# The up projection of a ConvFFN by Strassen's algorithm in a hybrid diffusion layer

## Chip, cores and metric

The kernel runs on one core of one Trainium2 chip. The metric is the device time of one execution in microseconds. Three runs of the kernel before have the median 1294.14 us (lowest 1293.99).

## What is computed

One layer of a diffusion backbone for 128 context tokens and 512 latent tokens, T = 640 columns in all: a combined input projection, latent attention beside a bidirectional state-space scan, their gated sum and an output projection, then a ConvFFN and a final norm. All numbers are fp32. The ConvFFN is the part that the change touches:

```
h2 = rmsnorm(x, lp['norm_ffn_g']) * (1 + sc2) + sh2
u = dwconv_centred(h2 @ lp['w_up'], lp['ffn_conv_w'], lp['ffn_conv_b'])
x = x + g2 * ((jax.nn.silu(u[..., :D_FF]) * u[..., D_FF:]) @ lp['w_down'])
```

with D_MODEL = 1024 and D_FF = 2816. The convolution has width 3 and runs along the tokens, within the context and within the latent tokens.

## The kernel before

Everything is feature-major: a tile has 128 features on the partitions and the 640 tokens as columns. A "page" is such a tile, 128x640.

**Products.** TensorE multiplies in the type fp32r. For accuracy each operand is split into a high and a low part, and `mm3` (L124) adds three products: high x high, high x low, low x high. `split` (L104) makes the parts: ScalarE (ACT) casts to the high part (L105), and VectorE (DVE) or GpSimd (POOL) subtracts it (`sub`, L101, shown in the profile as L102) for the low part. A product over 640 columns takes two matmuls, of 384 and 256 columns (`halves`, L131).

**Weights.** `wload` (L117) loads a raw weight tile of 128x1024 from the SP queue into one of four raw buffers and splits it, the low part on POOL, into one of two buffer pairs.

**ConvFFN, up.** w_up has 44 tiles of output features, in 22 pairs of a gate tile and a value tile. The loop (L1184) goes over the pairs. A tile is 8 steps of the contraction x 3 products x 2 halves = 48 matmuls into one PSUM buffer `big` of two banks (two such buffers); one value comes from `early_part` (L1165), a tile of the second pair that is computed ahead of its turn and lies in SBUF. `conv` (L451) evacuates: one ACT operation with the middle tap and the bias (L453), then four DVE operations for the two outer taps (L455, L458), of 127 and 511 columns, which read PSUM and the page they add to. Then ACT does SiLU (L1200), DVE multiplies the two halves (L1201) and `split` makes the two parts of the activation, which stay in SBUF (pools `fl`, `fr`).

**ConvFFN, down.** For each of 8 output tiles (L1209) 22 steps x 3 products x 2 halves = 132 matmuls are accumulated, and `residual` (L1090) adds the scaled result to x, which was parked in DRAM (`scr_x`). The last tile is done in two column parts (L1237), followed by the final norm and the stores.

**Ahead of it.** `h2_part` (L1142) makes the normed and modulated h2 in place in the tiles `x1` (fp32), and splits it into the pages `h2`, 16 of the 21 pages of pool `pg`.

**Order.** A planner orders the instructions of every engine by their priority in program order and by estimated durations; each engine then runs its own list strictly in that order. Only within `tc.manual_schedule` is the named engine's list the program order. DMAs of the weights, of x and of parked tiles all go through the SP queue.

Of the kernel before, what the change touches and what calls it, by code (L numbers as in the profile page):

```python
# [38 lines left out]
# steps of the streams of products with h between the parts of the attention (F_) and of the SSD (G_)  # L39
FILL0, F_R0, F_A0 = 16, 3, 4  # L40
F_S, F_P, F_R, F_Q, F_K = (0, 1, 1, 2), 1, 1, 1, 2
# start: buffers of modulation weights, and which feature tiles go to which engine at which step
# [9 lines left out]
# SSD: share of the other engines, buffers, and where the parts of decays() run  # L52
# [7 lines left out]
RP = 2  # L60
LAG, F_T, F_V = 2, (1, 2), (1, 0, 1, 1, 1)

# columns of the per-feature vector table
# [8 lines left out]
def trunk_kernel(ctx: ExitStack, tc: tile.TileContext, a: dict):  # L72
# [9 lines left out]
    def nm(s):  # L82
        uid[0] += 1
        return f"{s}{uid[0]}"
# [39 lines left out]
    def mm3(outs, hi, lo, rhs, first, last):  # L124
        """outs: list of (psum AP, column slice of the moving operand); rhs = (hi, lo)"""
        plan = [(hi, rhs[0]), (hi, rhs[1]), (lo, rhs[0])]
        for i, (w, r) in enumerate(plan):
            for o, s in outs:
                PE.matmul(o, w, r[:, s], start=first and i == 0, stop=last and i == 2)  # L129
# [20 lines left out]
    def sumsq(sqs, c):  # L150
        """PSUM column i: the sum over the features of the squares of token tile i of the columns c"""
# [17 lines left out]
    def rstd_rows(ps, n, c):  # L169
        """1 / rms of the tokens of the columns c on every partition, in PSUM; ps from sumsq"""  # L170
# [9 lines left out]
    def sqrt_table(x):  # L180
        """has the table of Sqrt loaded once x is there"""
# [4 lines left out]
    def rstd_full(sq, n, out, dg):  # L186
        """out [128, T]: 1 / rms from the sums of squares; dg: scratch [128, T]"""
# [7 lines left out]
    def add_sq(acc, x, sq):  # L195
        """acc + x * x"""
# [5 lines left out]
    def row_sums(stat, raws, m=128):  # L202
        """four partial sums each of the products of the columns stat (two rows, padded to 32) with the tiles raws"""
# [19 lines left out]
    def col_sums(ps, sb, m, n):  # L223
        """the partial sums added, feature-major"""
# [7 lines left out]
    def ada_rows(tiles, tile, nraw):  # L232
        """modulation columns by row products on the elementwise engines; tile(n) makes a [128, n] tile.
        tiles: the feature tiles. Returns a function that issues the next one of them behind an instruction of DVE"""
# [20 lines left out]
    def scale_col(out, sc, g):  # L255
        """(1 + sc) * g of one feature tile"""
        DVE.tensor_scalar(out, sc, 1.0, vec[:, g : g + 1], ALU.add, ALU.mult)

# [1 line left out]
    # the first columns of h @ w_in come from x * gain * (1 + scale) alone: the rms factors of the tokens and the  # L260
# [1126 lines left out]
```

## Time and profile before

| | |
|---|---|
| median of the runs | 1294.14 us |
| span of the profiled execution | 1293.0 us, 20744 instructions |
| PE (TensorE matmuls) busy | 1230.2 us, 95%, 8361 matmuls |
| PEld (weight loads) busy | 1165.6 us, 90% |
| DVE busy | 725.3 us, 56% |
| ACT busy | 542.7 us, 42% |
| POOL busy | 497.8 us, 38% |
| mean granted clock of TensorE | 0.975 |

The span runs from the first to the last instruction on the chip; some 1.1 us of the measured time lie outside it. Busy shares are averages over stages with different limits. An instruction that has started but is held up by something that no semaphore shows counts as busy, so that a mean duration can contain waiting. In the forms of the rows `128x640 f32<-128x640 f32` gives partitions x elements of output and input, and names such as `wlo<-raw,whi` the tiles written and read. `[2.30 <-DVE pg L458]` behind a row of the timeline is the idle time before it and what ended it.

### The profile page before, as it was taken

What the parts mean: (1) busy time and instruction counts of PE and PEld (TensorE: products, weight loads), DVE (VectorE), ACT (ScalarE), POOL (GpSimd) and SP (SyncE); (2) the same over time, 40 slices, a digit from 0 to 9 for tenths busy, and PEclk for the clock granted to TensorE, in tenths of its full rate; (3) what the DMA queues carried; (4) which work ended last, traced back from release to release, by engine and by line L of the source; (5) the groups of instructions that cost most, each with busy time, mean ns of one, the idle gap of its engine ahead of it and who ended that gap; (6) DMA issues with size and microseconds to landing.
All of it is one profiled execution on the core that took longest, in us unless ns stands there. A gap on an engine that the chain in (4) does not pass through costs nothing. (4 is left out here: it accounts for less than half of the span.)

```text
span 1293.0 us, 20744 instructions
## 1 busy us (share of the span) xinstructions
PE 1230.2 (95%) x8361; PEld 1165.6 (90%) x8361; DVE 725.3 (56%) x1285; ACT 542.7 (42%) x943; POOL 497.8 (38%) x260
## 2 busy tenths in 40 slices
PE   7798999999999889899989899999999999999997
PEld 5698999989999888788888898899999999999997
DVE  4767555564546895777788988744443443400003
ACT  5455454544547516535573231433333333311220
POOL 3433021221222236945577554323233332334450
PEclk9999999999999899999999988999999999999999
DMA  8333221222117764122356574121222222242212
GB/s 326 128 102 98 70 76 54 76 70 81 52 64 262 252 223 164 48 78 88 105 191 229 182 250 163 35 82 66 82 72 76 82 66 82 64 152 81 81 48 82
DMA packets 53680, 148.23 MB, mean 115 GB/s; under 512 B 6224, under 2 KB 11792, under 8 KB 53584
## 3 DMA queue, kind: packets, MB, share of 16 engines
q1 hardware_dynamic: 51824, 144.80, 33.3%
q10 hardware_dynamic: 1760, 2.11, 0.6%
q8 instruction: 66, 1.08, 0.4%
q14 instruction: 30, 0.25, 0.1%
HBM read 124.01 MB, written 20.35 MB: 112 GB/s over the span
## 5 line engine op out<-in xcount | busy, mean ns | idle before, releaser
L129 PE MATMUL big<-pg,whi 128*128 128x384 f32 (+1 forms) x3752 | 729.4, 315 | 6.6 <-DVE pg L1083 4.0
L129 PEld LDWEIGHTS big<-pg,whi 128*128 128x128 f32 x3752 | 572.2, 191 | 25.5 <-issue 16.4
L102 POOL TENSOR_TENSOR wlo<-raw,whi 128x1024 fp32r<-128x1024 f32 (+1 forms) x128 | 321.0, 2509 | 606.5 <-ACT whi L105 594.6
L129 PE MATMUL big<-pg,wlo 128*128 128x384 f32 (+1 forms) x1876 | 436.1, 312 | 6.5 <-POOL wlo L102 6.3
L129 PEld LDWEIGHTS big<-pg,wlo 128*128 128x128 f32 x1876 | 292.6, 191 | 8.4 <-POOL wlo L102 7.8
L105 ACT CAST whi<-raw 128x1024 fp32r<-128x1024 f32 (+2 forms) x133 | 135.1, 1016 | 189.4 <-PE big L129 169.1
L455 DVE SCALAR_TENSOR_TENSOR st<-big,vec,st 128x127 f32<-128x127 f32 x68 | 37.0, 544 | 105.3 <-ACT st L453 105.3
L105 ACT CAST pg<-pg 128x640 fp32r<-128x640 f32 x46 | 33.0, 727 | 106.6 <-DVE pg L1201 67.1
L1094 DVE SCALAR_TENSOR_TENSOR pg<-big,mod,pg 128x128 f32<-128x128 f32 (+2 forms) x15 | 7.5, 543 | 122.9 <-PE big L129 122.9
L129 PE MATMUL sm<-pg,whi 128*128 128x384 f32 (+1 forms) x256 | 63.0, 327 | 5.4 <-ACT pg L105 3.9
L102 DVE TENSOR_TENSOR pg<-pg,pg 128x640 fp32r<-128x640 f32 x43 | 41.1, 963 | 23.8 <-ACT pg L105 23.8
L129 PEld LDWEIGHTS sm<-pg,whi 128*128 128x128 f32 x256 | 46.0, 197 | 8.2 <-ACT pg L105 4.3
L250 DVE SCALAR_TENSOR_TENSOR araw<-araw,crow 128x1024 f32<-128x1024 f32 x32 | 52.6, 1645 | 0.4
L584 ACT ACTIVATE p<-sm,st 128x320 f32<-128x320 f32 x64 | 33.2, 524 | 44.7 <-DVE st L582 44.7
L455 DVE SCALAR_TENSOR_TENSOR pg<-big,vec,pg 128x127 f32<-128x127 f32 (+1 forms) x42 | 22.9, 545 | 51.4 <-ACT pg L453 51.4
L581 DVE TENSOR_REDUCE st<-sm 128x1 f32<-128x320 f32 (+1 forms) x72 | 31.6, 464 | 35.8 <-PE sm L577 35.7
L102 DVE TENSOR_TENSOR ptl<-sm,pth 128x512 fp32r<-128x512 f32 (+1 forms) x48 | 29.6, 621 | 37.1 <-ACT pth L600 37.0
L250 DVE SCALAR_TENSOR_TENSOR junk<-araw,crow 128x1024 f32<-128x1024 f32 x32 | 47.0, 1470 | 0.0
L600 ACT CAST pth<-sm 128x512 fp32r<-128x512 f32 (+1 forms) x48 | 25.5, 533 | 45.1 <-PE sm L597 44.9
L129 PE MATMUL sm<-pg,wlo 128*128 128x384 f32 (+1 forms) x128 | 41.3, 322 | 0.0
L458 DVE SCALAR_TENSOR_TENSOR st<-big,vec,st 128x127 f32<-128x127 f32 x68 | 37.2, 547 | 1.7
L998 DVE TENSOR_TENSOR k<-k,k 128x512 f32<-128x512 f32 x20 | 28.5, 1423 | 14.7 <-POOL k L997 12.6
(294 smaller groups left out, 1724.6 us busy)
## 6 DMA issues: line engine op xcount, KB each, us to landing
raw<-w_up SPq DMA_DIRECT2D x44, 512.0 KB, 3.3
araw<-w_adar SPq DMA_DIRECT2D x32, 512.0 KB, 4.6
araw<-w_ada SPq DMA_DIRECT2D x16, 512.0 KB, 7.8
raw<-w_down SPq DMA_DIRECT2D x14, 512.0 KB, 3.6
raw<-w_xbc SPq DMA_DIRECT2D x12, 512.0 KB, 3.4
raw<-w_gm SPq DMA_DIRECT2D x8, 512.0 KB, 3.3
raw<-w_o_mla SPq DMA_DIRECT2D x8, 512.0 KB, 3.4
raw<-w_z SPq DMA_DIRECT2D x8, 512.0 KB, 4.6
```

The costliest lines, as they stand in the source:

```text
L102: return eng.tensor_tensor(out, x, f(hi), ALU.subtract)
L105: ACT.copy(hi, src)
L129: PE.matmul(o, w, r[:, s], start=first and i == 0, stop=last and i == 2)
L250: DVE.scalar_tensor_tensor(out, raw, 1.0, crow[r], ALU.mult, ALU.mult, accum_out=mod[:, j, r : r + 1])
L455: DVE.scalar_tensor_tensor(dst[:, lo_ + 1 : hi_], p[:, lo_ : hi_ - 1], vec[:, w : w + 1], dst[:, lo_ + 1 : hi_], ALU.mult, ALU.add)
L458: DVE.scalar_tensor_tensor(dst[:, lo_ : hi_ - 1], p[:, lo_ + 1 : hi_], vec[:, w + 2 : w + 3], dst[:, lo_ : hi_ - 1], ALU.mult, ALU.add)
L581: DVE.reduce_max(st[:, i : i + 1], sv, AX.X)
L584: ACT.activation(p[:, i * w : (i + 1) * w], sv, AF.Exp, bias=st[:, 2:3], scale=SCALE, accum_out=st[:, 4 + i : 5 + i])
L600: return ph, pl, ACT.copy(ph[:, :n], pt[:, :n]), sub(DVE, pl[:, :n], pt[:, :n], ph[:, :n])
L998: DVE.tensor_tensor(w1, w1, e, ALU.mult)
L1094: ins = DVE.scalar_tensor_tensor(dst[:, lo_:hi_], ps[:, lo_ - cols.start : hi_ - cols.start], mod[:, gcol, r : r + 1], src[:, lo_:hi_], AL ...
```

## The change

In 20 of the 22 pairs of w_up (from the third on, `PLAIN` = 2) the product of a pair's 1024 x 256 weights with h2 is regarded as a 2x2 product of blocks: two blocks of 512 input features, two tiles of output features, and two halves of 320 tokens. Strassen's algorithm (in Winograd's form) makes the four output blocks from seven block products in place of eight. Each is 4 steps x 3 products of 320 columns, 12 matmuls.

- `t12`, `t34`: four sums of blocks of h2 (from `x1`), made once, split into pages of a pool `tt`.
- `seven(i)`: loads the two weight tiles of a pair, makes four sums of 128x512 on DVE and splits seven blocks of 128x512 (ACT cast, POOL subtraction) into buffers `sh`, `sl`, eight each. It is called one pair ahead.
- The seven products go into two banks of a `big` buffer and one bank of a `small`; products four to seven add to what an earlier product left there, after DVE or ACT has read it. Five DVE additions and two ACT copies of 320 columns make the gate tile `gt` and the value tile `vl` in SBUF pages, from which `conv` now reads.
- `gate`: after the product of the halves, the first four activations (`NKEEP`) are split into pages of the pool `xr`, which held `x1`; the next 17 go to DRAM, and the last stays as it is.
- w_down: its first three output tiles are computed together, in groups of four steps of the contraction; ahead of each group `act_split` loads the activations back and splits them. The other five tiles are as before.

```
+PLAIN, NKEEP = 2, 4
...
+    xr = ctx.enter_context(tc.tile_pool(name="xr", bufs=8))
...
-        x = hp_.tile([128, T], F32, tag="x1", name=nm("x1"), bufs=8)
+        x = page(F32, xr)
...
+    N2 = T // 2
+    lft, rgt = slice(0, N2), slice(N2, T)
+    ffn = ExitStack()
+    tt = ffn.enter_context(tc.tile_pool(name="tt", bufs=16))
+    sw = ffn.enter_context(tc.tile_pool(name="sw", bufs=1))
+    def gate(i, us):
+        ACT.activation(us[0], us[0], AF.Silu)
+        DVE.tensor_tensor(us[0], us[0], us[1], ALU.mult)
+        if i < NKEEP:
+            hi, lo = page(F32R, xr), page(F32R, xr)
+            split(hi, lo, us[0])
+            act[i] = (hi, lo)
+        elif i < NF - 1:
+            d = tc.dram_tile([128, T], F32, name=f"scr_act{i}")
+            nc.sync.dma_start(d, us[0])
+            act[i] = d
+        else:
+            act[i] = us[0]
...
+    for i in range(PLAIN):
...
+    t12, t34 = [], []
+    for k in range(4):
+        b1, b2 = x1[k], x1[4 + k]
+        ta, tb = page(), page()
+        DVE.tensor_tensor(ta[:, lft], b1[:, rgt], b1[:, lft], ALU.subtract)
+        DVE.tensor_tensor(ta[:, rgt], b2[:, rgt], ta[:, lft], ALU.subtract)
+        POOL.tensor_tensor(tb[:, lft], b2[:, rgt], b1[:, rgt], ALU.subtract)
+        DVE.tensor_tensor(tb[:, rgt], b2[:, lft], ta[:, rgt], ALU.subtract)
+        for t, out, eng in ((ta, t12, DVE), (tb, t34, POOL)):
+            hi, lo = page(F32R, tt), page(F32R, tt)
+            split(hi, lo, t, eng)
+            out.append((hi, lo))
+    def half_w():
+        return [sw.tile([128, 512], F32R, tag=t, name=nm(t), bufs=8) for t in ("sh", "sl")]
+    def part():
+        return sw.tile([128, N2], F32, tag="o3", name=nm("o3"), bufs=5)
+    def seven(i):
+        raw = []
+        for j in range(2):
+            r_ = ws.tile([128, 1024], F32, tag="raw", name=nm("raw"), bufs=RAW)
+            nc.sync.dma_start(r_, a["w_up"][2 * i + j])
+            raw.append(r_)
+        (a11, a12), (a21, a22) = ((r_[:, 0:512], r_[:, 512:1024]) for r_ in raw)
+        out = []
+        def add(x, y, op):
+            t = sw.tile([128, 512], F32, tag="sum", name=nm("sum"), bufs=4)
+            DVE.tensor_tensor(t, x, y, op)
+            return t
+        def put(x):
+            hi, lo = half_w()
+            split(hi, lo, x, POOL)
+            out.append((hi, lo))
+        put(a11)
+        s1 = add(a21, a22, ALU.add)
+        s2 = add(s1, a11, ALU.subtract)
+        put(s2)
+        put(add(a11, a21, ALU.subtract))
+        put(s1)
+        put(a12)
+        put(add(a12, s2, ALU.subtract))
+        put(a22)
+        return out
+    def product(ps, w, b, c, first):
+        for k in range(4):
+            s = slice(k * 128, (k + 1) * 128)
+            mm3([(ps, c)], w[0][:, s], w[1][:, s], b[k], first and k == 0, k == 3, not first)
+    h2a, h2b = h2[:4], h2[4:]
+    with tc.manual_schedule(engines={PE.engine}):
+        nxt = seven(PLAIN)
+        for i in range(PLAIN, NF):
+            w11, ws2, ws3, ws1, w12, ws4, w22 = nxt
+            if i + 1 < NF:
+                nxt = seven(i + 1)
+            ab, c = big(), small()[:, 0:N2]
+            pa, pb = ab[:, 0:N2], ab[:, 512 : 512 + N2]
+            gt, vl = page(), page()
+            product(pa, w11, h2a, lft, True)
+            p1 = part()
+            ACT.copy(p1, pa)
+            product(pb, ws2, t12, rgt, True)
+            u2 = part()
+            DVE.tensor_tensor(u2, pb, p1, ALU.add)
+            product(c, ws3, t34, lft, True)
+            product(pb, ws1, t12, lft, False)
+            u4 = part()
+            DVE.tensor_tensor(u4, pb, p1, ALU.add)
+            DVE.tensor_tensor(vl[:, rgt], c, u4, ALU.add)
+            product(pa, w12, h2b, lft, False)
+            ACT.copy(gt[:, lft], pa)
+            product(pb, ws4, h2b, rgt, False)
+            DVE.tensor_tensor(gt[:, rgt], pb, p1, ALU.add)
+            product(c, w22, t34, rgt, False)
+            DVE.tensor_tensor(vl[:, lft], c, u2, ALU.add)
+            us = []
+            for j, p in enumerate((gt, vl)):
+                u = stage() if j else page()
+                conv(u, p, V_FW + 3 * (2 * i + j), V_FB + 2 * i + j)
+                us.append(u)
+            gate(i, us)
+    ffn.close()
+    fl = ctx.enter_context(tc.tile_pool(name="fl", bufs=34))
+    def act_split(i):
+        if i < NKEEP:
+            return
+        x = act[i]
+        if i < NF - 1:
+            x = page()
+            nc.sync.dma_start(x, act[i])
+        hi, lo = (page(F32R, fl if i < NKEEP + 17 else pg) for _ in range(2))
+        split(hi, lo, x)
+        act[i] = (hi, lo)
...
+    with tc.manual_schedule(engines={PE.engine}):
+        pss = [halves(big()), halves(big()), [(small()[:, 0:HALF], slice(0, HALF)), (small()[:, 0 : T - HALF], slice(HALF, T))]]
+        for k0 in range(0, NF, 4):
+            n = min(4, NF - k0)
+            for k in range(k0, k0 + n):
+                act_split(k)
+            for m in range(3):
+                hi, lo = wload(a["w_down"][m][:, k0 * 128 : (k0 + n) * 128], n * 128)
+                for k in range(n):
+                    s = slice(k * 128, (k + 1) * 128)
+                    mm3(pss[m], hi[:, s], lo[:, s], act[k0 + k], k0 + k == 0, k0 + k == NF - 1)
```

## Rows read from the trace of the kernel before

**Rows 1.** The chain of waits in order of time: start, us, what.

```profile
837.71 423.47 PE big L129 x2892
```

**Rows 2.** Busy time by stretch: length, PE, PEld, DVE, ACT, POOL, PEclk, DMA, GB/s.

```profile
950.00:1000.00 50.00, 50.00 (x343) 50.00 (x342) 19.70 (x34) 18.31 (x22) 16.82 (x7) 1.00 0.22 74
1150.00:1200.00 50.00, 50.00 (x345) 50.00 (x344) 2.02 (x4) 9.22 (x10) 18.99 (x10) 1.00 0.35 110
```

**Rows 3.** Timeline of ACT in w_up: start, us, instruction, idle before and its releaser.

```profile
957.44 1.05 ACT L105 CAST whi<-raw 128x1024 fp32r<-128x1024 f32 x1 [2.16 <-PE big L129]
...
971.52 1.05 ACT L105 CAST whi<-raw 128x1024 fp32r<-128x1024 f32 x1 [2.16 <-PE big L129]
```

**Rows 4.** Timeline of TensorE in the attention: twelve matmuls of 320 columns.

```profile
308.23 0.46 PE L129 MATMUL sm<-cqh,pg 128*128 128x320 f32 x2
...
309.98 0.75 PE L129 MATMUL big<-pg,whi 128*128 128x384 f32 x4
```

**Rows 5.** Timeline of POOL at the start of w_up.

```profile
834.35 2.41 POOL L102 TENSOR_TENSOR wlo<-raw,whi 128x1024 fp32r<-128x1024 f32 x1 [2.08 <-ACT whi L105]
837.39 2.38 POOL L102 TENSOR_TENSOR wlo<-raw,whi 128x1024 fp32r<-128x1024 f32 x1 [0.64 <-ACT whi L105]
```

**Rows 6.** Timeline of POOL in the scan.

```profile
540.50 2.48 POOL L997 TENSOR_TENSOR k<-k,k 128x512 f32<-128x512 f32 x2
...
545.12 1.60 POOL L997 TENSOR_TENSOR k<-k,k 128x512 f32<-128x512 f32 x1 [0.69 <-DVE k L990]
547.23 2.50 POOL L102 TENSOR_TENSOR wlo<-raw,whi 128x1024 fp32r<-128x1024 f32 x1 [0.50 <-ACT whi L105]
```

**Rows 7.** Timeline of DVE in the scan (sm is PSUM).

```profile
544.90 0.68 DVE L998 TENSOR_TENSOR k<-k,k 128x512 f32<-128x512 f32 x1
545.50 1.40 DVE L987 TENSOR_TENSOR k<-k,sm 128x256 f32<-128x256 f32 x4
...
547.78 2.50 DVE L998 TENSOR_TENSOR k<-k,k 128x512 f32<-128x512 f32 x1 [0.28 <-ACT k L988]
```

**Rows 8.** Timeline of DVE in w_up: convolutions from PSUM (big) and SBUF (pg).

```profile
835.48 0.35 DVE L458 SCALAR_TENSOR_TENSOR pg<-big,vec,pg 128x127 f32<-128x127 f32 x1
...
837.49 2.43 DVE L458 SCALAR_TENSOR_TENSOR pg<-pg,vec,pg 128x127 f32<-128x127 f32 x1
...
952.27 0.35 DVE L455 SCALAR_TENSOR_TENSOR pg<-big,vec,pg 128x127 f32<-128x127 f32 x1 [2.38 <-ACT pg L453]
...
953.69 0.75 DVE L458 SCALAR_TENSOR_TENSOR pg<-big,vec,pg 128x511 f32<-128x511 f32 x1
```

**Rows 9.** Groups by line and form in w_up: busy, mean ns, idle before.

```profile
L1201 DVE TENSOR_TENSOR pg<-pg,st 128x640 f32<-128x640 f32 x19 | 15.7, 826 | 0.7
L102 DVE TENSOR_TENSOR pg<-pg,pg 128x640 fp32r<-128x640 f32 x19 | 15.7, 826 | 15.1 <-ACT pg L105 15.1
```

**Rows 10.** Timeline of DVE around the output projections.

```profile
733.30 2.23 DVE L251 TENSOR_SCALAR mod<-mod,vec 128x2 f32<-128x2 f32 x1
...
740.17 2.19 DVE L251 TENSOR_SCALAR mod<-mod,vec 128x2 f32<-128x2 f32 x1
```

**Rows 11.** Timeline of POOL in the same stretch.

```profile
732.03 3.48 POOL L102 TENSOR_TENSOR wlo<-raw,whi 128x1024 fp32r<-128x1024 f32 x1 [3.40 <-ACT whi L105]
```

**Rows 12.** DMA issues: count, KB each, median us to landing.

```profile
pg<-scr_gs SPq DMA_DIRECT2D x8, 320.0 KB, 5.7
```

**Rows 13.** Timeline of TensorE behind an idle time.

```profile
744.76 0.58 PE L129 MATMUL sm<-pg,whi 128*128 128x384 f32 x1 [3.94 <-ACT pg L105]
...
746.69 0.63 PE L129 MATMUL sm<-pg,whi 128*128 128x256 f32 x2
...
747.33 0.63 PE L129 MATMUL sm<-pg,whi 128*128 128x256 f32 x2
```

**Rows 14.** Busy time by stretch, columns as in the second group.

```profile
712.00:716.00 4.00, 0.92 (x6) 0.69 (x6) 3.93 (x6) 0.00 (x0) 1.54 (x1) 1.00 0.13 17
...
746.00:750.00 4.00, 4.00 (x18) 4.00 (x19) 3.96 (x8) 0.52 (x1) 0.00 (x0) 0.50 0.85 324
```

More of the change, by code (lines that the diff above doesn't have):

```diff
@@ L122, in wload, with mm3 @@
         return hi, lo
-    def mm3(outs, hi, lo, rhs, first, last):
+    def mm3(outs, hi, lo, rhs, first, last, on=False):
         plan = [(hi, rhs[0]), (hi, rhs[1]), (lo, rhs[0])]
@@ L128, in mm3 @@
             for o, s in outs:
-                PE.matmul(o, w, r[:, s], start=first and i == 0, stop=last and i == 2)
+                PE.matmul(o, w, r[:, s], start=first and i == 0, stop=last and i == 2, skip_group_check=on)
     def halves(ps):
@@ L1180, in trunk_kernel @@
     mst.close()
-    fl = ctx.enter_context(tc.tile_pool(name="fl", bufs=28))
-    fr = ctx.enter_context(tc.tile_pool(name="fr", bufs=14, side="right"))
-    act = []
-    for i in range(NF):
+    N2 = T // 2
[16 more added lines that the diff above has]
+            act[i] = us[0]
+    act = [None] * NF
+    for i in range(PLAIN):
         us = []
@@ L1199, in trunk_kernel @@
             us.append(u)
-        ACT.activation(us[0], us[0], AF.Silu)
-        DVE.tensor_tensor(us[0], us[0], us[1], ALU.mult)
-        fp = fl if i < 14 else fr if i < 21 else pg
-        hi, lo = page(F32R, fp), page(F32R, fp)
-        split(hi, lo, us[0])
-        act.append((hi, lo))
-    x2 = []
+        gate(i, us)
[11 more added lines that the diff above has]
+            out.append((hi, lo))
@@ new lines, in product @@
+    def product(ps, w, b, c, first):
[34 more added lines that the diff above has]
+                us.append(u)
+            gate(i, us)
@@ L1211, in trunk_kernel @@
         nc.sync.dma_start(x, x1d[m])
+        sq = acc if m == 0 else stage()
+        if m < 3:
+            for o, c in pss[m]:
+                residual(x, o, 40 + m, x, c)
+            ACT.activation(sq, x, AF.Square)
+            if m:
+                POOL.tensor_tensor(acc, acc, sq, ALU.add)
+            x2.append(x)
+            continue
         last = m == 7
@@ L1226, in trunk_kernel @@
                     mm3(outs, hi[:, s], lo[:, s], act[k0 + k], k0 + k == 0, k0 + k == NF - 1)
-        sq = acc if m == 0 else stage()
         if not last:
```

## Prediction

> **What bounds the kernel now.** I read the chain of waits first, from its end backwards. From 837.7 us to 1261 us it is a single piece: 423.5 us of matmuls of the helper `mm3` (L129) with nothing between them [rows 1]. That stretch is the ConvFFN, and TensorE alone sets its length. The busy times by stretch say the same: in the w_up stage TensorE is busy for 50.0 of 50 us at granted clock 1.00, VectorE (DVE) for 19.7, ScalarE (ACT) for 18.3 and GpSimd (POOL) for 16.8; in the w_down stage DVE has 2.0 [rows 2]. The pace is read from the casts of successive weight tiles, which wait for TensorE: two tiles, one pair, take 971.52 - 957.44 = 14.08 us [rows 3], and a pair is 96 matmuls, so 147 ns each at 320 columns on average. Fewer matmul columns shorten this stage as long as nobody else becomes slower than TensorE. So what has to be read next is how much room the others have, above all DVE and POOL, which get the block sums.
>
> **TensorE's part.** A Strassen product is 4 x 3 = 12 matmuls of 320 columns. The trace has twelve of that width in a row: they start at 308.23 and the next form starts at 309.98, 1.75 us [rows 4]. Seven products are 12.25 us a pair against 14.08. Over 20 pairs that is 36.6 us less, if TensorE still sets the pace.
>
> **POOL's part.** Before: two subtractions of 1024 columns a pair, 2.4 us each [rows 5]. After: `put` runs seven of 512. Two POOL operations of 512 columns with nothing in their way took 2.48 us [rows 6], so 1.24 each and 8.7 us a pair.
>
> **DVE's part.** Per pair, with nothing in its way: four sums of 512 (two such operations start 0.60 apart [rows 7]) 2.4 us; two convolutions, 2.17 each (952.27 to 953.69 + 0.75 [rows 8]) 4.3; the product of the halves, 0.83 [rows 9]; five additions of 320 columns from PSUM, put at 0.42 each from four of 256 in 1.40 us [rows 7], 2.1. The split of 0.83 [rows 9] leaves the loop except in two pairs. Together 9.6 us. ACT goes from 18.3 per 50 us, 5.2 a pair, to some 7.4: less two casts of 1.05 [rows 3] and one of 0.73, plus seven half casts at 0.6 and two copies at 0.4. Taken one by one, no engine reaches 12.25.
>
> **DVE and POOL cannot be taken one by one.** A DVE sum of 512 elements, both inputs in SBUF, starts at 547.78 and takes 2.50 us instead of 0.68; POOL has an operation from 547.23 to 549.73, and the DVE operation ends 0.55 us behind it [rows 6, 7]. The other way, POOL's operation at 545.12 takes 1.60 us, 0.36 over its 1.24, while DVE's of 544.90 finishes. But four DVE operations that read PSUM run at 0.35 us each beside POOL (545.50). The stage at issue has the same twice. The convolution of the early tile, which lies in SBUF, needs 2.43 us for 127 columns (837.49) while POOL works from 837.39 to 839.77; the same line reading PSUM needs 0.35 beside POOL's work of 834.35 [rows 5, 8]. So a DVE operation with two SBUF inputs and a POOL operation take turns, whole instructions at a time.
>
> The Trainium skill, "SBUF — State Buffer", section "SBUF: two separate sides", calls the port pair that the two engines share an exclusive lock, held for a whole instruction. By that rule alone the pair would come to the second of the bounds below; the rows above agree with it.
>
> Before, this costs nothing: POOL works 2.4 us per tile, and the convolutions read PSUM. The change moves both convolutions onto SBUF pages (`gt`, `vl`), adds four SBUF sums, and raises POOL from 4.8 to 8.7 us. Of DVE's 9.6 us, 7.5 now need the turn and 2.1 (the PSUM additions) don't. Bounds for the pair's time:
> - lowest: only the data passes count. 0.55 us for 512 elements [rows 6, 7] gives 5.6 us for the 5240 elements of a pair; with POOL's 8.7 that is 14.3 us.
> - all PSUM additions lie beside POOL's work: 7.5 + 8.7 = 16.2 us.
> - as in the w_out stage, where DVE is never idle: each turn of 6.87 us (733.30 to 740.17) holds one POOL operation of 2.4 us, and DVE stands about 2.1 us of it at a 128x2 operation that takes 2.23 [rows 10, 11]. That is 87%: 9.6 + 0.87 x 8.7 = 17.2 us.
> - nothing overlaps: 18.3 us.
>
> I take 16.7, between the second and the third, because DVE reaches a PSUM addition at 5 of 18 operations only. That is 2.6 us a pair over 14.08, and 20 pairs make **+52.4 us** where the arithmetic alone promised -36.6. TensorE waits in the fourth and sixth product, whose PSUM half must first be read by DVE's `u2` and `u4`; behind them in its queue stand the remaining products. Who is late next is ACT (it casts a weight when a product has freed its buffer) and then POOL.
>
> **The rest.** The two pairs that still split their activations in the loop: 2 x 0.83 = +1.7 us on DVE. Ahead of the loop, `t12` and `t34` need 12 DVE sums of 320 (about 0.41 each, half of a 640 [rows 9]), 4 DVE splits (0.83), 4 POOL sums (0.8) and 4 POOL splits (1.5): 17.5 us of turns, beside three plain tiles with 7.2 us of POOL, 3.3 of gates, a convolution from SBUF and the first weights, 32 us in all against the 22.9 us of three tiles and one product. Between nothing and 10 us of that is late; I take **+6**, since the first turns begin ahead of the tiles' end. Into w_down, `fl` takes over the memory of `tt` and `sw`, so its splits start after the last product; the four activations kept in `xr` give TensorE 4 x 3 x 6 matmuls, 10.5 us, of cover, against DVE's last convolutions and gate (5.2), four splits (3.3) and three POOL weights that take turns with them (3.7): **+2**, ends 0 and 5. Inside w_down a group of four steps asks 3.3 us of DVE and 3.7 of POOL per 10.5 us of matmuls, and DVE had 2.0 of 50 us to do [rows 2]: nothing, and if that cover went, at most those 7 us per group. The activations go out and come back in 17 DMAs of 320 KB each way; such a load lands in 5.7 us [rows 12], with a pair or a group of time for each. On the SP queue a store waiting for its gate holds up the loads behind it, but four raw buffers are two pairs of slack: nothing.
>
> **The sum** is made against the profiled execution: span 1293.0 us, the median of the runs 1294.14, so 1.1 us lies around it. 1294.1 + 52.4 + 1.7 + 6 + 2 = **1356 us**, 4.8% more. The forecast's own range, with 15.5 to 17.7 us a pair and the ends of the rest, is 1324 to 1383.
>
> **Rivals.**
> *TensorE stays the bound (faster).* For this, DVE must stand still for less than 12.25 - 9.6 = 2.65 us of POOL's 8.7 us. That is the point that decides. It speaks for it that every engine by itself is below 12.25; against it, that only 2.1 us of DVE's work can lie beside POOL, and that none of the operations in [rows 5 to 8] escaped its turn. Time: 1294 - 36.6 + 6 + 2 = 1265 us. The Trainium skill, "Perfetto Trace Analysis", section "Identifying the Most-Contended Engine", finds the bound by the highest occupancy of a single engine; by that rule it would be this one. Chance 0.13.
> *The turns interleave without loss (no change).* DVE's start-up lies wholly inside POOL's turns, 14.3 us a pair: 1294 + 4.4 + 1.7 + 6 + 2 = 1308 us. For it: DVE ended 0.55 us after POOL, less than its 0.68. Against: the in-order queue of DVE also holds its waits for ACT and TensorE. Chance 0.17.
> *The waits lower TensorE's clock (much slower).* After an idle time of 3.94 us the granted clock was 0.50, the 1.2 GHz level, and three matmuls of 256 columns took 0.64 us [rows 13, 14], 213 ns each, so 267 for 320 and 22.4 us for seven products. A stretch with 3.1 of 4 us idle kept 1.00 [rows 14]. With 4.4 us idle a pair, gathered in one gap, about half of a pair would run low: 19.5 us, 1294 + 108 + 10 = 1412 us. Spread over two or three waits the gaps are shorter than those that the clock survived. Chance 0.10.
>
> **Numbers.** Forecast 0.60, rivals 0.13, 0.17, 0.10. The range 1290 to 1400 holds the forecast, the second rival and the low end of the third, 0.8 together, and leaves out the first. Over 2%, about what a measurement of this kernel can tell from no change, is beyond 1320 or below 1268: slower 0.70 (forecast and third rival), within 0.17, faster 0.13.
>
> **What would show it.** In the changed kernel: the pitch of a pair 16 to 17 us, not 12.3; TensorE busy for about 75% of the loop with gaps that end at DVE's `u2` or `u4`; the mean of DVE's 512-wide sums and of the convolutions' 127-wide operations far above 0.68 and 0.35; POOL's 512-wide subtractions at 1.3 to 1.9; clock 1.00. Wrong it would be if these means stay at 0.68 and 1.24, or if TensorE's gaps end at ACT or a DMA.

## The result: slower, 1408 us

The changed kernel takes **1408.33 us** (median of four runs, 1406.44 to 1409.79) against 1294.14 us of the kernel before in the same session (1293.99 to 1296.33): ratio **1.088, 95% interval 1.0866 to 1.0893**. A fourth run of the kernel before took 1673.71 us and is left out as a slow one. The sign was forecast; the forecast's 1356 us was 52 us too low, and 1408 lies outside its range. The profiled execution has a span of 1406.6 us, 113.6 us over the span before. All line numbers are now a few higher: L131 is the matmul, L107 the cast, L104 the subtraction, L1258 the block sums, L1296 ACT's copy `p1`, L1299 `u2`, L1303 `u4`, L1306 ACT's copy into `gt`, L1304 and L1310 the two sums into `vl`, L455 the convolution's ACT part, L457 and L460 its DVE parts, L1195 the product of the halves.

The pace first. In every kernel with a Strassen loop the gate's product on DVE occurs once a pair, so two of them give the pitch. Timeline of DVE after the change, the sixth and the eighteenth:

```profile
944.07 0.81 DVE L1195 TENSOR_TENSOR pg<-pg,st 128x640 f32<-128x640 f32 x1
...
1168.60 0.82 DVE L1195 TENSOR_TENSOR pg<-pg,st 128x640 f32<-128x640 f32 x1
```

Twelve pairs take 224.53 us: **18.71 us a pair**, against 14.08 before [rows 3] and 16.7 forecast. Twenty pairs are 20 x 4.63 = 92.6 of the 113.6 us; the other 21.0 are put down to the loop's two ends.

Busy time by stretch, the answer to [rows 2]:

```profile
950.00:1000.00 50.00, 37.02 (x225) 34.91 (x224) 30.51 (x49) 20.50 (x34) 25.27 (x18) 0.95 0.22 77
```

TensorE has fallen from 50.0 to 37.0 of 50 us. But **nobody has taken its place**: DVE is busy for 61%, POOL for 51%, ACT for 41%. No engine's busy time sets this pace; waits do. The longest, of the sixteen pairs between 900 and 1200 us (waits: us in total, times, longest):

```profile
POOL sl L104 <- ACT sh L107: 139.4, 108, 5.0
ACT sh L107 <- PE big L131: 104.9, 49, 6.1
DVE sum L1258 <- POOL sl L104: 96.3, 47, 4.9
...
PE big L131 <- ACT o L1296: 38.3, 16, 2.7
...
PE big L131 <- DVE o L1303: 26.1, 16, 3.3
```

It goes round: DVE waits for POOL, POOL for ACT, ACT for TensorE, and TensorE for ACT and DVE. TensorE's three gaps of one pair, from its timeline:

```profile
1005.83 0.56 PE L131 MATMUL big<-pg,sh 128*128 128x320 f32 x2 [1.36 <-DVE o L1303]
...
1008.79 0.56 PE L131 MATMUL big<-pg,sh 128*128 128x320 f32 x2 [0.94 <-ACT pg L1306]
...
1016.72 0.57 PE L131 MATMUL big<-pg,sh 128*128 128x320 f32 x2 [2.37 <-ACT o L1296]
```

These are the starts of the **fifth, the sixth and the second** product. Compare what they write with what they wait for. The fifth writes `pa` and waits until `u4` has read `pb`; the sixth writes `pb` and waits for the copy of `pa`; the second writes `pb` and waits for the copy of `pa`. Each waits for a reader of the *other* half of `ab`: `pa` and `pb` are slices of one two-bank tile, and the program's waits are made for the tile.

The second product's 2.37 us can be followed into ACT's list (timeline):

```profile
1014.00 0.92 ACT L455 ACTIVATE st<-pg,vec 128x640 f32<-128x640 f32 x1 [0.86 <-DVE pg L1310]
1014.82 0.60 ACT L107 CAST sh<-sum 128x512 fp32r<-128x512 f32 x1
1015.61 0.74 ACT L1194 ACTIVATE pg<-pg 128x640 f32<-128x640 f32 x1 [0.19 <-DVE pg L460]
1016.26 0.41 ACT L1296 COPY o<-big 128x320 f32<-128x320 f32 x1
```

The first product had ended at about 1014.3. Its copy stands behind the convolution and the Silu of the pair before, and these wait for DVE.

The turns of DVE and POOL are there as well, but not everywhere (groups by line and form in 900 to 1000; the second number behind the bar is the mean in ns):

```profile
L457 DVE SCALAR_TENSOR_TENSOR st<-pg,vec,st 128x511 f32<-128x511 f32 x6 | 10.5, 1753 | 0.0
...
L460 DVE SCALAR_TENSOR_TENSOR pg<-pg,vec,pg 128x127 f32<-128x127 f32 x5 | 4.9, 972 | 0.0
...
L460 DVE SCALAR_TENSOR_TENSOR st<-pg,vec,st 128x511 f32<-128x511 f32 x6 | 4.4, 738 | 0.0
L1258 DVE TENSOR_TENSOR sum<-raw 128x512 f32<-128x512 f32 x6 | 4.1, 678 | 0.0
...
L1258 DVE TENSOR_TENSOR sum<-raw,sum 128x512 f32<-128x512 f32 x5 | 3.5, 692 | 18.9 <-POOL sl L104 18.9
```

One 511-wide operation takes 1.75 us where its twin takes 0.74, and one 127-wide operation 0.97 where [rows 8] have 0.35; but three of the four block sums run at the free 0.68 to 0.69 us. DVE and POOL stand so long in waits that they collide at a few places only.

### The profile page after: what moved, and what is told of

It is laid out like the page before. It is cut to its first block, busy times and chain, and to the rows that moved or that the text cites. A ratio compares the mean times of both kernels' runs of the same rounds, so it can differ in the third digit from the quotient of the medians.

```text
span 1406.6 us, 21108 instructions
## 1 busy us (share of the span) xinstructions
PE 1237.2 (88%) x8121; PEld 1154.2 (82%) x8121; DVE 868.2 (62%) x1484; ACT 608.6 (43%) x1100; POOL 619.2 (44%) x377
## 5 line engine op out<-in xcount | busy, mean ns | idle before, releaser
L131 PE MATMUL big<-pg,whi 128*128 128x384 f32 (+1 forms) x2384 | 477.4, 320 | 7.8 <-DVE pg L1085 4.4
L104 POOL TENSOR_TENSOR wlo<-raw,whi 128x1024 fp32r<-128x1024 f32 (+3 forms) x97 | 231.4, 2389 | 428.0 <-ACT whi L107 420.8
L131 PEld LDWEIGHTS big<-pg,whi 128*128 128x128 f32 x2384 | 370.4, 193 | 26.7 <-issue 17.5
L131 PE MATMUL big<-pg,wlo 128*128 128x384 f32 (+1 forms) x1192 | 283.1, 316 | 10.5 <-POOL wlo L104 10.4
L131 PE MATMUL big<-pg,sh 128*128 128x320 f32 x800 | 192.1, 327 | 99.4 <-ACT o L1296 44.4
L131 PEld LDWEIGHTS big<-pg,sh 128*128 128x128 f32 x800 | 137.1, 195 | 116.3 <-ACT o L1296 49.7
L131 PEld LDWEIGHTS big<-pg,wlo 128*128 128x128 f32 x1192 | 189.6, 194 | 12.9 <-POOL wlo L104 12.3
L104 POOL TENSOR_TENSOR sl<-sum,sh 128x512 fp32r<-128x512 f32 x80 | 109.8, 1374 | 121.2 <-ACT sh L107 120.4
L107 ACT CAST whi<-raw 128x1024 fp32r<-128x1024 f32 (+3 forms) x102 | 94.7, 929 | 99.7 <-PE big L131 67.1
L131 PE MATMUL big<-pg,sl 128*128 128x320 f32 x400 | 127.9, 320 | 0.0
L104 POOL TENSOR_TENSOR sl<-raw,sh 128x512 fp32r<-128x512 f32 x60 | 86.8, 1447 | 46.2 <-ACT sh L107 45.9
L107 ACT CAST sh<-sum 128x512 fp32r<-128x512 f32 x80 | 49.0, 615 | 129.4 <-PE big L131 99.7
L131 PE MATMUL sm<-pg,whi 128*128 128x384 f32 (+1 forms) x344 | 80.4, 325 | 7.9 <-DVE pg L104 2.5
L131 PEld LDWEIGHTS big<-pg,sl 128*128 128x128 f32 x400 | 78.8, 197 | 0.0
L131 PE MATMUL sm<-pg,sh 128*128 128x320 f32 x320 | 78.5, 335 | 0.0
L131 PEld LDWEIGHTS sm<-pg,whi 128*128 128x128 f32 x344 | 60.0, 198 | 10.9 <-DVE pg L104 3.3
L107 ACT CAST sh<-raw 128x512 fp32r<-128x512 f32 x60 | 37.0, 619 | 62.1 <-POOL sl L104 32.2
L104 DVE TENSOR_TENSOR pg<-pg,pg 128x640 fp32r<-128x640 f32 (+2 forms) x55 | 52.4, 973 | 16.9 <-ACT pg L107 16.9
L107 ACT CAST pg<-pg 128x640 fp32r<-128x640 f32 x54 | 37.9, 724 | 56.0 <-DVE pg L1086 35.6
L131 PEld LDWEIGHTS sm<-pg,sh 128*128 128x128 f32 x320 | 61.2, 214 | 0.0
L1258 DVE TENSOR_TENSOR sum<-raw,sum 128x512 f32<-128x512 f32 x20 | 14.4, 718 | 64.4 <-POOL sl L104 64.4
```

The costliest lines, as they stand in the source:

```text
L104: return eng.tensor_tensor(out, x, f(hi), ALU.subtract)
L107: ACT.copy(hi, src)
L1258: DVE.tensor_tensor(t, x, y, op)
```

## The experiments

The pitch is read as above, from the sixth and eighteenth gate; the clock is that of 950 to 1000 us. "Own banks" means that `pa`, `pb` and `c` are separate PSUM tiles. "Free banks" means that the fourth and sixth product also write tiles of their own.

| kernel | time, us | pitch, us | clock |
|---|---|---|---|
| changed kernel | 1408.3 | 18.71 | 0.95 |
| e1 own banks | 1387.7 | 18.19 | 0.86 |
| e2 shared tile, no subtractions | 1372.8 | 17.04 | 1.00 |
| e3 own banks, no subtractions | 1275.7 | 12.32 | 1.00 |
| e5 own banks, subtractions on DVE | 1350.1 | 16.21 | 0.93 |
| e6 own banks, POOL's turns without their results | 1311.5 | 13.73 | 1.00 |
| e8 own banks, convolution later | 1371.2 | 17.07 | 0.90 |
| e9 free banks | 1364.1 | 17.09 | 0.86 |
| e10 free banks, 5 of 7 subtractions on DVE | 1305.2 | 13.65 | 1.00 |
| e11 free banks, 7 of 7 on DVE | 1310.8 | 13.78 | 0.97 |
| e14 changed kernel, gaps filled | 1402.2 | 18.12 | 1.00 |
| e15 own banks, gap filled | 1361.9 | 16.34 | 1.00 |

The kernel before took 1292.05 to 1295.15 us in these sessions (medians). e2, e3, e5, e6, e8, e9 and e11 are single runs; four runs of one of the other kernels lie within 2 to 5 us of each other. e2, e3 and e6 compute other numbers than the layer.

**The shared tile and the subtractions, each alone and both (e1 to e3), and the rest of the change alone (e4).** e1:

```
-            ab, c = big(), small()[:, 0:N2]
-            pa, pb = ab[:, 0:N2], ab[:, 512 : 512 + N2]
+            pa, pb, c = big()[:, 0:N2], small()[:, 0:N2], small()[:, 0:N2]
```

> The accumulators pa and pb get a PSUM buffer each instead of one two-bank buffer; nothing else changes. Theory W (TensorE waits three times a pair, 4.7 us, because a write to one bank of a shared buffer is held until the readers of the other bank are done): the waits for ACT's copy p1 before the second product, for DVE's u4 before the fifth and for ACT's copy of gt before the sixth go, a pair falls from 18.7 to 14 to 15 us, the time from 1408 to 1315 to 1335 us. Theory T (DVE and POOL take turns on SBUF, the forecast's): a pair can't go below 16.2 us, so at most 50 us come back, 1358 us or more; TensorE's waits only move to u2 and u4.

e2 leaves POOL's seven subtractions out; the products use the high part of a weight also where the low part belongs, so the count of matmuls stays:

```
-            hi, lo = half_w()
-            split(hi, lo, x, POOL)
-            out.append((hi, lo))
+            hi = sw.tile([128, 512], F32R, tag="sh", name=nm("sh"), bufs=8)
+            ACT.copy(hi, x)
+            out.append((hi, hi))
```

> The seven POOL subtractions of a pair are left out of the loop (the low part of a Strassen weight is the high part's tile, so the products are computed from other numbers); the shared PSUM buffer stays. Theory T: with POOL's 8.7 us a pair gone, DVE needs 9.6 us, a pair falls to TensorE's 12.3 to 14 us, the time to 1310 us or less. Theory W: the three waits of TensorE stay, since they hang on ACT's and DVE's order and on the shared buffer; only their length shrinks where DVE stood behind POOL, a pair to 16 to 17 us, the time to 1350 to 1375 us.

e3 has both edits.

> Both edits: a PSUM buffer each for pa and pb, and no POOL subtractions in the loop (low part of a Strassen weight = its high part's tile, other numbers). Both theories: TensorE is the bound at 12.3 us a pair, the loop takes 250 us, the time is 1265 to 1285 us. What it lies below the first of these runs is what the turns of DVE and POOL still cost there: theory T says 60 us or more, theory W 30 to 50 us.

e4 keeps only the way of the activations and w_down, with all 22 pairs plain (`PLAIN` = 22, no `t12`, `t34`).

> All 22 pairs of w_up as before the change, with the activations by way of DRAM and the first three tiles of w_down together: the last part of the change alone. From the changed kernel's trace, w_down takes 174 us against 164 before, with two waits of 3.9 and 1.8 us for POOL and a clock of 0.91 behind them. If that is the new w_down's own cost, this kernel takes 1300 to 1305 us; if it came from the late Strassen loop (DVE's and POOL's lists behind), it takes 1294 to 1297 us.

e4 took 1296.47 us over ten runs, ratio 1.0028 (1.0008 to 1.0047): the DRAM and w_down parts cost about 3 us by themselves, and Strassen's part has the rest. In e3 the arithmetic's promise is met: 12.32 us a pair, TensorE busy for 50.0 of 50 us. But the two edits **do not add**. e1 by itself looks like the case for the turns, e2 by itself like the case for the shared tile: own banks alone win 20.7 us (ratio to the kernel before 1.0725, 1.0707 to 1.0742), the missing subtractions alone 35.6, both together 132.7. e3 lies 112 us below e1 and 97 below e2. Either cause alone suffices to hold the loop near its pace. In e2, where no engine waits for POOL any more, TensorE still stands at the same three places, 42.6 us in 12 pairs (waits of TensorE in 900 to 1100):

```profile
PE big L131 <- ACT o L1296: 23.2, 12, 1.9
PE big L131 <- ACT pg L1306: 12.4, 12, 1.0
PE big L131 <- DVE o L1303: 7.0, 12, 0.6
```

In e1 the three gaps have become one. The timelines of DVE and of TensorE in it:

```profile
1003.85 1.65 DVE L460 SCALAR_TENSOR_TENSOR pg<-pg,vec,pg 128x127 f32<-128x127 f32 x2
...
1005.42 2.05 DVE L457 SCALAR_TENSOR_TENSOR st<-pg,vec,st 128x127 f32<-128x127 f32 x2
...
1007.39 3.02 DVE L460 SCALAR_TENSOR_TENSOR st<-pg,vec,st 128x127 f32<-128x127 f32 x2
1010.33 0.48 DVE L1298 TENSOR_TENSOR o<-sm,o 128x320 f32<-128x320 f32 x1
```

```profile
1010.86 0.90 PE L131 MATMUL sm<-pg,sh 128*128 128x320 f32 x2 [3.67 <-DVE o L1298]
...
1014.23 0.73 PE L131 MATMUL big<-pg,sh 128*128 128x320 f32 x2
```

This is the wait that the prediction had named: the fourth product may not add to `pb` until `u2` (here L1298) has read it. `u2` stands in DVE's list behind the previous pair's convolutions, stretched by turns (a 127- and a 511-wide one take 3.02 us where 1.00 is free). Behind the gap the fourth product takes 14.23 - 10.86 = 3.37 us instead of the 1.75 of [rows 4]; the granted clock of that stretch is 0.50, the 1.2 GHz level.

**What of POOL's part counts (e5, e6), and the place of the convolution (e8).** e5 gives all seven subtractions to DVE (`split(hi, lo, x, DVE)`, own banks).

> Own banks, and all seven weight subtractions of a pair on DVE instead of POOL: no work is left out, POOL is idle in the Strassen loop. Theory T (the turns of DVE and POOL hold the loop once the shared buffer is gone): DVE's own work is 9.3 us a pair in the kernel without subtractions, plus 7 x 0.69 = 14.1 us, with nobody to take turns with; 20 pairs x (14.1 - 12.3) above its 1275.7 give 1312, range 1300 to 1335, and DVE's 511-wide convolution ops stay at 0.75 us. Theory L (the length of DVE's list ahead of the sum u2, not the turns, holds it): the list is longer by 4.8 us a pair, so the gap before the fourth product stays at 3 us or more and the time at 1370 or above.

e6 keeps POOL's turns and takes their results out of everybody's way:

```
+            hi = sw.tile([128, 512], F32R, tag="sh", name=nm("sh"), bufs=14)
+            jk = sw.tile([128, 512], F32, tag="jk", name=nm("jk"), bufs=1)
+            ACT.copy(hi, x)
+            POOL.tensor_tensor(jk, f(hi), f(hi), ALU.subtract)
+            out.append((hi, hi))
```

> Own banks; the low part of each weight tile is left out (the products use the high part in its place), and POOL does a subtraction of the same shape instead whose result nobody reads, seven a pair, with 14 buffers for the high parts so that its lateness holds up nobody: the subtractions' turns remain, their chain (cast, subtraction, product; subtraction, sum's buffer) is gone. Theory T (turns): DVE's ops with two SBUF inputs and POOL's still add up to some 15.6 us a pair and u2 still stands behind stretched convolutions: 1345 to 1395. Theory C (what counts is the chain through POOL, that is sums and products that wait for its results): 1275 to 1295, as without the subtractions.

e5 and e6 came out between their expectations. In e6 the turns alone cost 13.73 - 12.32 = 1.41 us a pair. Of the 18.19 - 12.32 = 5.87 us that POOL's subtractions cost in e1, the other 4.46 thus come with others waiting for their results, or with the fewer buffers (e6 has 14 for the high parts, e1 has eight); no run separates these two. The turns show plainly where POOL works without pause. First POOL, then DVE, from their timelines:

```profile
993.56 7.26 POOL L1265 TENSOR_TENSOR jk<-sh 128x512 f32<-128x512 f32 x5 [2.29 <-ACT sh L1264]
...
994.24 1.26 DVE L1195 TENSOR_TENSOR pg<-pg,st 128x640 f32<-128x640 f32 x1
995.42 1.52 DVE L1258 TENSOR_TENSOR sum<-raw 128x512 f32<-128x512 f32 x1
997.04 1.36 DVE L1258 TENSOR_TENSOR sum<-sum,raw 128x512 f32<-128x512 f32 x1
998.32 0.48 DVE L1304 TENSOR_TENSOR o<-sm,o 128x320 f32<-128x320 f32 x1
...
999.24 0.68 DVE L1258 TENSOR_TENSOR sum<-raw,raw 128x512 f32<-128x512 f32 x1
```

Two of DVE's block sums from SBUF double to 1.36 and 1.52 us, while the operation from PSUM keeps its 0.48. So the turns are real. On this the exclusive lock of the Trainium skill ("SBUF — State Buffer", "SBUF: two separate sides") and the trace agree in kind. They do not add up as whole instructions, though: in these 7.26 us POOL does five operations and DVE four with two SBUF inputs, 5 x 1.24 + 0.83 + 3 x 0.60 = 8.8 us at the prediction's prices, so parts of them overlap. And e6's 13.73 us lie below the lowest bound of the prediction, 14.3.

e5 has no turns, DVE's 511-wide operations are back at 0.74 us, and it still takes 16.21 us a pair: turns cannot be all.

e8 puts the convolutions of a pair behind `u4` and the third output sum of the next one in DVE's list, so that `u2` no longer stands behind them; DVE's list is the program order there, like TensorE's.

> Own banks, and the convolution and gate of a pair stand in DVE's list behind u2, u4 and the third output sum of the next pair; all work and POOL's seven subtractions stay. Theory L (the place of u2 behind the convolutions holds the loop): TensorE no longer waits at the fourth product, the pitch falls to 16 us or below and the time to 1290 to 1345, with the clock back at 1.00. Theory T in its strict form (the sum of the turns holds it wherever they stand): the pitch stays at 16.2 us or more, the time at 1345 to 1390, and TensorE's gaps move to another sum or to the casts.

Neither theory fitted. Time and pitch (1371, 17.07) lie where the strict turns had them, but the gap did not move to another sum: TensorE still waits for `u2`, 35.5 us in 11 pairs, and now DVE waits too (waits of DVE in 900 to 1100):

```profile
DVE o L1311 <- PE sm L131: 42.0, 12, 3.7
```

That is `u4` (here L1311), waiting 3.5 us a pair for the fourth product, with the convolutions queued behind it. This gave the third theory, called K in the next expectations: **the loop is a cycle.** The fourth product waits for `u2`, `u4` waits for the fourth product, and the whole of DVE's list lies between `u4` and the next `u2`. A pair then takes DVE's stretched list *plus* its waits for TensorE.

**Cutting the cycle (e9 to e11).**

```
+            pb4, pb6 = small()[:, 0:N2], small()[:, 0:N2]
...
-            product(pb, ws1, t12, lft, False)
+            product(pb4, ws1, t12, lft, True)
             u4 = part()
-            DVE.tensor_tensor(u4, pb, p1, ALU.add)
+            DVE.tensor_tensor(u4, pb4, u2, ALU.add)
...
-            product(pb, ws4, h2b, rgt, False)
-            DVE.tensor_tensor(gt[:, rgt], pb, p1, ALU.add)
+            product(pb6, ws4, h2b, rgt, True)
+            DVE.tensor_tensor(gt[:, rgt], pb6, u4, ALU.add)
```

> The fourth and sixth products get PSUM buffers of their own (the sums become u4 = P4 + u2 and gt.r = P6 + u4, as many DVE ops as before), so no product writes a buffer that u2, u4 or the p1 copy must have read within the same pair, but for the fifth and seventh; all work and POOL's seven subtractions stay. Theory K (the loop is a cycle through TensorE and DVE: P4 waits for u2, u4 waits for P4, and DVE's list with POOL's turns and its own waits stands between one u2 and the next): the wait of 3.2 to 3.7 us at the fourth product goes, the clock is 1.00, and what is left is DVE's stretched list, 13.5 to 15 us a pair: 1300 to 1335. Theory T in its strict form (turns alone add up to over 16 us): 1345 to 1390 and the gap moves to another product.

> As e9, with five of the seven weight subtractions on DVE and two on POOL (those of the blocks a11 and a12). By the turns as one sum, DVE 9.3 + 5 x 0.69 = 12.75 us a pair, and ops that take turns some 12.8: with theory K the pair takes 12.8 to 14.2 us and the time is 1285 to 1320, at or a little below the kernel before at best. If DVE's waits for the casts inside its list (1.3 us a pair in the run with all seven on DVE) stay, 1310 to 1340.

> As e9, with all seven subtractions on DVE and POOL idle in the loop: no turns. Theory K: 9.3 + 4.8 = 14.1 us of DVE a pair and no cycle through TensorE: 1310 to 1325, against 1350 with the fourth product in u2's buffer. If the bank sharing was not what coupled them: 1340 to 1355 as there.

Where there are no turns, K held: e11 takes 1310.8 where e5, its twin with `u2` and the fourth product in one tile, takes 1350.1. e10 at 1305.2 (ratio 1.0084, 1.0067 to 1.0101) lies in its range. With all turns (e9) K's range was missed: 1364.1 is where the strict sum of turns had it, and the gap moved to another product, as that theory had it, too. Busy times by stretch of e9 and of e10:

```profile
950.00:1000.00 50.00, 39.50 (x233) 38.71 (x231) 45.28 (x56) 20.31 (x34) 28.90 (x21) 0.86 0.24 83
```

```profile
950.00:1000.00 50.00, 45.74 (x307) 44.69 (x306) 49.86 (x85) 26.16 (x44) 11.40 (x8) 1.00 0.31 104
```

In both an engine is at last near its limit: DVE, busy for 45.3 of 50 us in e9 and for 49.9 in e10. In e9 this is 0.906 x 17.09 = 15.5 us of DVE a pair, where e3's pair without turns has 37.50 of 50 us, 9.2 us. With the cycle cut, TensorE waits at one place only, the seventh product, for the sum into `vl` (L1304, 38.7 us in 12 pairs). **e9 comes nearest to the kernel that the prediction had described**: DVE's list, stretched by turns, fills most of the pair, 17.09 us against the 16.7 taken and the bounds 16.2 and 17.2. It does not prove that sum. For 1.6 of the 17.09 us DVE stands idle, and e6 has the same seven POOL operations a pair:

```profile
950.00:1000.00 50.00, 46.79 (x307) 44.68 (x306) 45.36 (x67) 26.82 (x45) 36.05 (x27) 1.00 0.28 100
```

There DVE is busy for 45.36 of 50 us, 12.5 us a pair, not 15.5. Three of its four 511-wide convolution operations take 1.26 to 1.32 us in e9 on average (934 to 1071 us); in e6 all four take 0.74 to 0.83. Over the 9.2 us of e3, seven POOL operations stretch DVE's pair by 6.3 us in e9 and by 3.3 in e6; the prediction's sum has one price for both. Whether e9 with more than eight buffers for the weights' parts would come nearer to e6 was not tried.

**The prelude (e12, e13).** Ahead of the loop TensorE waits 8 us for `t12` and `t34`, also in e10. e12 puts the fifth and sixth product of the first pair right behind its first one; e13 has three plain pairs (`PLAIN` = 3); both on e10.

> As e10 (own banks, five subtractions on DVE, two on POOL), and in the first Strassen pair alone the fifth and sixth products, which read h2 and not its differences, come right after the first. In e10 TensorE waits 8.0 us for the differences t12 and t34 in 851 to 862, and its clock is at half for some 7 us behind the gap. If this prelude is what e10 still loses, the two products (3.5 us of work) take some of the wait's place: 3 to 7 us less, 1298 to 1302. If DVE, 100% busy from there on, only passes the lateness on into the loop: 1304 to 1307, no change.

> As e10, with three plain pairs ahead of nineteen Strassen pairs: one pair more at 14.08 in place of 13.3 us (+0.8), during which t12 and t34 can be made beside TensorE's work. If the prelude's wait (8.0 us and the half clock behind it) goes: 1296 to 1300. If the differences are made as late as before, against the plain pairs' own convolutions on DVE: 1304 to 1310.

e12 took 1303.91 (ratio 1.0094, 1.0066 to 1.0122), no change from e10's 1305.21 that the runs can tell. Its waits for `t12` and `t34` fall from 8.0 to 4.8 us, but DVE is full behind them (8.00 of 8 us from 862 on), and TensorE's waits for the first sum into `vl` rise from 3.6 to 5.4 us between 845 and 905. e13 took 1309.33 (1.0132, 1.0106 to 1.0159); there the differences are still late, and TensorE waits 12.4 us for them.

**The clock (e14, e15).** A recorded rival had given 1412 us by way of the lowered clock, 4 us from the result, so it had to be tested and not read off. Matmuls that nobody reads keep TensorE at work in its gaps:

```
+    def fill(n):
+        for _ in range(n):
+            PE.matmul(junk, h2[0][0][:, 0:128], h2[0][0][:, lft], start=True, stop=True)
```

> The changed kernel with matmuls that nobody reads in TensorE's three gaps of a pair: 14 ahead of the second product, 9 ahead of the fifth, 5 ahead of the sixth (0.146 us each at full clock), into a buffer of their own; no work is left out and the lists of the other engines are as they were but for two pairs of neighbours. Clock theory (the half clock behind the gaps, 0.95 in the stage, lengthens the products that the cycle runs through): the clock goes to 1.00 and the time falls by 10 to 30 us, to 1378 to 1398. Theory K (the cycle is made of other engines' lists and of the shared buffer; TensorE's products have room): the clock rises and the time stays within 8 us of 1408.

> The kernel with own banks (1387.65, e1) with 18 matmuls that nobody reads ahead of the fourth product, in its gap of 3.7 us a pair, into a buffer of their own. There the fourth product itself runs at half clock (its first matmuls take 0.80 us for three in place of 0.44), and u4 waits for it. If that product's length is in the cycle, it gets up to 1.3 us a pair shorter: 1362 to 1375. If the half clock is harmless there too: 1380 to 1395.

In both the clock went to 1.00. In the changed kernel this is worth 1408.3 - 1402.2 = 6 us (ratio to the kernel before 1.0833, 1.0798 to 1.0868, from 1.088, 1.0866 to 1.0893; the intervals just touch), within what theory K allowed. By the pitch it would be 20 x 0.59 = 11.8 us; about half of that is lost again in the first and last four pairs. In e1 it is worth 1387.7 - 1361.9 = **26 us** (1.0523, 1.0495 to 1.0551). There one gap of 3.67 us precedes exactly the product that the cycle runs through. The timeline of TensorE in e15:

```profile
1002.91 0.55 PE L131 MATMUL sm<-pg,sh 128*128 128x320 f32 x2 [1.09 <-DVE o L1304]
...
1004.77 0.46 PE L131 MATMUL big<-pg,sh 128*128 128x320 f32 x2
```

The fourth product takes 1.86 us instead of 3.37, 1.51 less, and the pitch falls by 1.85. Over 20 pairs that is 37 us; the loop's ends take 11 of them back.

## Why the prediction was wrong

**TensorE's part** was right: 12.25 us a pair was forecast, and e3 has 12.32 with TensorE never idle. The forecast's busy share of about 75% came out, too (74%), but over other gaps, and the clock of 1.00 did not (0.95).

**The turns** exist; e6 shows the doubling in single rows. Their price was not right as a sum of whole instructions: e6 runs a pair in 13.73 us, under the lowest bound of 14.3. That e9 comes out at 17.09, near the 16.7, is partly luck, since DVE stands idle for 1.6 us of it, which the sum did not have. The rule of the busiest single engine, in the Trainium skill's "Perfetto Trace Analysis", section "Identifying the Most-Contended Engine", would have named TensorE, as the rival at 1265 did. Only e3, without subtractions and without the shared tile, comes near that time (1275.7).

**The step that failed** is the sentence on the waits: "TensorE waits in the fourth and sixth product, whose PSUM half must first be read by DVE's `u2` and `u4`; behind them in its queue stand the remaining products." It put the waits at the wrong products and, above all, at no cost of their own, as if the sum of turns were the pair: 16.7 us against 18.71. In the changed kernel TensorE waits ahead of the second, fifth and sixth product, for readers of the other half of `ab`. Two of the three releasers are ACT's copies, which the prediction had costed at nothing beyond ACT's busy time. I had read `pa` and `pb` as two banks; the program waits by tiles. The sign of being wrong, "or if TensorE's gaps end at ACT or a DMA", was the right alarm: 38.3 us of gaps in 16 pairs end at `p1`. Of the 52 us by which the forecast was too low, 20 x (18.71 - 16.7) = 40 lie in the pairs and 11 at the loop's ends.

What it cost follows from cutting the coupling in two steps. Separate tiles for `pa` and `pb` give 1408.3 to 1387.7; separate tiles for the fourth and sixth product give 1387.7 to 1364.1. So **44 us, 1.62 us a pair and some 12 us at the ends,** are coupling, with POOL's subtractions in place; without them the shared tile alone costs 97 us (e2 to e3). The second hides behind the first, which is why the first cut alone bought so little.

**The ends of the loop** come to 21.0 us in the changed kernel, against 6 + 2 + 1.7 = 9.7 forecast; in e9 to 1364.1 - 1294.1 - 20 x 3.01 = 9.8. What the trace of the changed kernel shows of them, in TensorE's timeline:

```profile
852.28 0.57 PE L131 MATMUL big<-pg,sh 128*128 128x320 f32 x2 [0.89 <-ACT o L1296]
855.79 0.63 PE L131 MATMUL big<-pg,sh 128*128 128x320 f32 x1 [2.65 <-DVE pg L104]
861.02 0.63 PE L131 MATMUL big<-pg,sh 128*128 128x320 f32 x1 [4.07 <-DVE pg L104]
862.18 0.64 PE L131 MATMUL big<-pg,sh 128*128 128x320 f32 x1 [0.26 <-ACT pg L107]
863.90 0.63 PE L131 MATMUL big<-pg,sh 128*128 128x320 f32 x1 [1.08 <-DVE pg L104]
...
1245.54 0.90 PE L131 MATMUL big<-pg,wlo 128*128 128x384 f32 x2 [3.92 <-POOL wlo L104]
```

The first Strassen pair stands 9.0 us for `p1`, `t12` and `t34` (6 were taken for the prelude, between 0 and 10), and w_down waits 5.2 us for POOL's splits in two waits, one of 3.92 (2 were taken, between 0 and 5). e9 stands 9.2 us for the differences and 4.1 us in w_down, so it hits the forecast's 9.7 with other parts: luck. Where it is better than the changed kernel is read from the gates, first four of e9 (the second, the sixth, the eighteenth and the last), then the second and the last of the changed kernel:

```profile
857.62 1.48 DVE L1195 TENSOR_TENSOR pg<-pg,st 128x640 f32<-128x640 f32 x1
...
934.58 1.52 DVE L1195 TENSOR_TENSOR pg<-pg,st 128x640 f32<-128x640 f32 x1
...
1139.71 1.52 DVE L1195 TENSOR_TENSOR pg<-pg,st 128x640 f32<-128x640 f32 x1
...
1194.57 0.82 DVE L1195 TENSOR_TENSOR pg<-pg,st 128x640 f32<-128x640 f32 x1
```

```profile
857.41 1.48 DVE L1195 TENSOR_TENSOR pg<-pg,st 128x640 f32<-128x640 f32 x1
...
1238.41 0.81 DVE L1195 TENSOR_TENSOR pg<-pg,st 128x640 f32<-128x640 f32 x1
```

The last four pairs take 54.9 us in e9, 13.5 less than four of its pitches, and 69.8 in the changed kernel, only 5.0 less. The first four take 8.6 and 11.8 us more than four pitches. So 8.5 of the 11.2 us between the two lie in the last pairs and some 3 in the first. e9's DVE sets its pace and has no block sums left to make in the last pair; that this is the reason was not tested.

**The clock rival** had the number, by luck, and not the reason. It wanted one gap of 4.4 us a pair and half of each pair at 1.2 GHz. The changed kernel has three gaps of 2.37 us and less and a stage clock of 0.95; filling them returns 6 us of 114. In e1, where there is one gap, the rival's mechanism does work, at 26 us.

**The sum again**, with what was measured: 1294.1 + 20 x (17.09 - 14.08) for a pair with all tiles apart (e9) = 1354.3; + 20 x (18.71 - 17.09) for the coupling = 1386.7; + 21.0 for the ends = 1407.7, against 1408.3. It has to close, since the ends are what was left over; what the experiments add is the split. How e9's 17.09 splits further, into turns and waits for POOL's results, is open beyond e6's 1.41 us.

No version that does all the work beats the kernel before. e10 runs its pairs in 13.65 us, below 14.08, which gives back 20 x 0.43 = 8.6 us; its ends take that and 11 us more. How much of those ends a better order could save beyond e12 and e13 stays open.

## What to carry to other kernels

When work moves from a saturated engine to two that share something, look at the waits as a graph before adding busy times. If a product must wait for a reader that stands in an in-order list, and that list in turn waits for the product, the period is the list plus the waits, whatever the busiest engine's share. Give accumulators that are read half-way tiles of their own, not slices of one: here it was worth 44 us of 1408. And undo suspects in pairs: of two that hold the same loop, each alone looks small.

## What the hardware showed that I had not expected

- A gap in front of the very product that the cycle runs through costs more than its length: 3.67 us of idle time lengthened that product from 1.86 to 3.37 us (e15 and e1), and matmuls without any use made the kernel 26 us faster.
- A subtraction on POOL was dearer for DVE than doing it there. From e3 to e11, which has free banks, too, seven subtractions on DVE add 13.78 - 12.32 = 1.46 us a pair, since DVE had room; from e11 to e9 the same seven on POOL add 3.31 more. e11's row has DVE busy for 46.90 of 50 us, 12.9 us a pair with the subtractions; e9 has 15.5 without them.

```profile
950.00:1000.00 50.00, 47.70 (x310) 46.72 (x309) 46.90 (x89) 26.10 (x43) 0.00 (x0) 0.97 0.30 101
```
